# A paired feed-forward block: the chain behind a pair's products takes a step more, and SyncE's requests at the second group's start change places

## The chip, the cores and the metric

One NeuronCore of a Trainium2 chip runs the whole program in one launch. The metric is the device time of one execution in microseconds; for the kernel before, three runs gave a median of 971.46 us (970.23 to 972.13). Engines are named as in the profile: PE is TensorE (PEld its weight loads), DVE is VectorE, ACT is ScalarE, POOL is GpSimd, SP is SyncE, which here only issues DMAs.

## The reference

A macaron layer on 512 tokens of width 1024, in fp32: a feed-forward half step, a token mixer (differential and dilated attention), a second feed-forward half step, and a norm.

```
def swiglu(x, w_gate, w_up, w_down):
    return (jax.nn.silu(x @ w_gate) * (x @ w_up)) @ w_down
...
x = x + 0.5 * swiglu(rmsnorm(x, ffn1_norm[layer]), ffn1_w_gate[layer], ffn1_w_up[layer], ffn1_w_down[layer])
x = x + token_mixer(rmsnorm(x, mix_norm[layer]), ...)
x = x + 0.5 * swiglu(rmsnorm(x, ffn2_norm[layer]), ffn2_w_gate[layer], ffn2_w_up[layer], ffn2_w_down[layer])
return rmsnorm(x, final_norm)
```

The hidden width is 2816, that is 22 tiles of 128. The change lies in the two feed-forward stages alone; stage a is the first (its tiles end in a), stage b the second.

## The kernel before

**Numbers.** Every fp32 operand of a product is split into a high part, rounded to TensorE's fp32r format by a cast on ScalarE (`high`, L382), and a low part, the rest, made by a subtraction on VectorE (`low`, L386). A product of two operands is then three matmuls (`mm3`, L123 to L125): high by high, high by low, low by high.

**Tiles in pairs.** Of the 22 hidden tiles the first six (stage a) or four (stage b) are computed one at a time. From there two neighbours form a pair, and a pair's gate, its up product and later two tiles of the down product are each done with seven block products instead of eight, after Strassen and Winograd. One block product is twelve matmuls of 128x256. The seven of a unit and the PSUM bank that each writes (w, x, y or z) are the list `SEVEN`:

```
SEVEN = (("a11", "w", "b11"), ("s3", "z", "t3"), ("s2", "x", "t2"), ("a12", "w", "b21"),
         ("s1", "y", "t1"), ("a22", "x", "t4"), ("s4", "y", "b22"))
```

The weights' blocks a11, a12, a22 come from raw tiles (raw0, raw1). The sums s1 and s3 are formed by DMA: SyncE loads one block into a slot and GpSimd issues a second DMA that adds the other to it (`weight_sums`, L327). The sums s2 and s4 are VectorE's (`total`, L358). The blocks' own sums are carried through PSUM: after a11 ScalarE copies bank w into x, after s2 bank x into y (`product`, `put(starts[t + 1], A.copy, ...)`, in the profile at L411), and the later products add to them. So s1 can't start before the copy x to y is done. The block s4 writes y again, so it can't start before VectorE has read y for the second row (L414).

**Units.** `units` lists a stage's work in TensorE's order: the first gate pair, then gate and up of each further pair up to tile 12, five plain tiles of the down product ("p", over the unpaired tiles), the down product's first group of four units ("d"), then the pairs 14 to 20 (the second group), three plain tiles and the second group of d.

**The order of the other engines.** TensorE's order follows the list. VectorE's and ScalarE's (and SyncE's and GpSimd's in these stages) is written by a small event queue: every operation is put on a heap with a planned time and a rank, and the heap is emptied in order of time, then rank, then entry. A block product is planned at 1410 ns (`STEP`), a plain tile at 4080 ns. The planned times only make the order; on the chip each engine runs its list in order and waits on semaphores.

**Around a pair.** `pair_step` (L461) puts what follows each block. In a gate unit, ScalarE applies silu to bank w for g0's left half (after a12), VectorE adds to make both halves of g1 (after s1 and a22), ScalarE applies silu to g1 and to g0's right half. In the up unit VectorE multiplies g0 and g1 by the up product. g0 and g1 lie in a pool of two buffers (`ptb`), so the next pair's g0 takes the buffer of this one's and must wait for its last readers.

**The chain of T blocks.** `kept` (L499) turns a pair's g0 and g1 into what the down product reads. b11 and b2 are plain splits of g0's left half and of g1 (tiles h0, and h1 and h2). The T blocks need differences, made in place: two subtractions on g0 (`less`, L420), two on g1 (`stt`, L423), the second of each after the first. Then g0 is cast (tile h3, L550) and split (h4), and g1 is cast (h5, L558, called the second cast here) and split (h6). These run while TensorE is in the next pair's gate unit.

**Loads.** `pipeline` plans `weight_sums` of a unit 14 steps ahead of it and `load` (raw tiles, three buffers in rotation) seven steps ahead; where both fall on one time, the sums' rank is the lower and they come first. The sums lie in slots that the hidden tiles use too; those of gate 16 take slots that tile h2's rest and another of pair 8 held until the last unit of the first group d has read them.

Of the kernel before, what the change touches and what calls it, by code (L numbers as in the profile page):

```python
# [14 lines left out]
F32 = mybir.dt.float32  # L15
F32R = mybir.dt.float32r
I32 = mybir.dt.int32
AF = mybir.ActivationFunctionType
ALU = mybir.AluOpType
AX = mybir.AxisListType  # L20

P = 128
S = 512
# [20 lines left out]
PLAIN = 6  # L44
# [10 lines left out]
STEP, PLAIN_STEP = 1410, 4080  # L55
# [9 lines left out]
def tile_macaron(ctx: ExitStack, tc, xs, xT, wf, wgu1, wst1, wd1, wdg1, wqk, wv, wo, wgu2, wst2, wd2,  # L65
                 wdg2, lams, relb, onehot, addc, out):
    nc = tc.nc
    V, A, G, T = nc.vector, nc.scalar, nc.gpsimd, nc.tensor
# [4 lines left out]
    tp = ctx.enter_context(tc.tile_pool(name="tp", bufs=2))  # L73
# [124 lines left out]
    def ffn(wgu, wst, wd, wdg, n0, n1, norm, early, res, nm, hooks, ended, first=None,  # L198
# [90 lines left out]
        ups, up_w = {}, {}  # L289
        left, right = slice(0, HS), slice(HS, S)  # L290
# [11 lines left out]
        ops, begin, starts, now = [], {}, [], 0  # L302
# [25 lines left out]
        sums, raws, second, made, half, g, hs = {}, {}, {}, {}, [], {}, {}  # L328
# [72 lines left out]
        def at(time, rank, f, *a):  # L401
            count[0] += 1
            heapq.heappush(events, (time, rank, count[0], f, a))

        def put(time, f, *a):
            at(time, 0, f, *a)
# [6 lines left out]
        def add(o, a, b):  # L413
            V.tensor_tensor(o, a, b, op=ALU.add)  # L414

        def mul(o, a, b):
            V.tensor_tensor(o, a, b, op=ALU.mult)
# [46 lines left out]
        def pair_step(t, u, o, banks):  # L464
            j = u[1]
            pw, px, py, pz = (banks[b] for b in "wxyz")
            p7 = (sq if u[0] == "u" else res["bc"])[:, left]
            if o == "s3":
                put(t, A.copy, p7, pz)
            elif u[0] == "g":  # L470
                if o == "a12":
                    def first_block():
                        g[j] = [tp.tile([P, S], F32, tag="ptb", name=f"g{r}{nm}{j}")
                                for r in range(2)]
                        A.activation(g[j][0][:, left], pw, AF.Silu)

                    put(t, first_block)
                    if j == n1:
                        put(t + STEP, lambda: mul(g[j][0][:, left], ups[j][:, left],
                                                  g[j][0][:, left]))  # L480
                    return
                if o == "s2":
                    return
                g0, g1 = g[j]
                if o == "s1":
                    put(t, add, g1[:, right], py, p7)
                elif o == "a22":
                    put(t, add, g1[:, left], px, p7)
                    put(t + STEP * (j > n1),
                        lambda: A.activation(g1[:], g1[:], AF.Silu, scale=-1.0))  # L490
                elif o == "s4":
                    put(t, A.activation, g0[:, right], py, AF.Silu)
                    if j == n1:
                        put(t, mul, g1[:], ups[j + 1][:], g1[:])
                        put(t + STEP, mul, g0[:, right], ups[j][:, right], g0[:, right])
                        kept(j, t, t - 2 * STEP, t + STEP)
            else:
                g0, g1 = g[j]
                if o == "a12":  # L499
                    put(t, mul, g0[:, left], pw, g0[:, left])  # L500
                elif o == "s1":
                    put(t, add, sq[:, right], py, p7)
                elif o == "a22":
                    put(t, add, sq[:, left], px, p7)
                    put(t, stt, g1[:], sq[:], -1.0, g1[:], ALU.mult)
                elif o == "s4":
                    put(t, mul, g0[:, right], py, g0[:, right])
                    kept(j, t - STEP, t - 3 * STEP, t)

        def kept(j, t1, t0, t2):  # L510

            g0, g1 = g[j]

            def cast(o, a):
                A.copy(o, a)

            def rest(o, a, h):
                V.tensor_tensor(o, a, h.bitcast(F32), op=ALU.subtract)  # L520

            def parts(t, h, l, a):
                put(t, cast, h, a)
                put(t + STEP, rest, l, a, h)

            if j < PLAIN:
                for r, t in ((1, t1), (0, t2)):
                    h = ah[j + r] = slot(j + r, f"ah{nm}{j + r}", F32R)
                    l = al[j + r] = slot(JF + j + r, f"al{nm}{j + r}", F32R)
                    parts(t + STEP, h[:], l[:], g[j][r][:])  # L530
                return
            places = [lambda n=n, i=i: slot(i, f"h{n}{nm}{j}", F32R)
                      for n, i in enumerate(PAIR_SLOTS[(j - PLAIN) // 2 % 4])]
            t = {}

            def b11():
                t["b"] = places[0]()
                A.copy(t["b"][:, left], g0[:, left])

            def b2():  # L540
                t["h2"] = places[1]()
                A.copy(t["h2"][:], g1[:])

            def b2_rest():
                t["l2"] = places[2]()
                rest(t["l2"][:], g1[:], t["h2"][:])

            def t0_parts():
                t["h0"] = places[3]()
                A.copy(t["h0"][:], g0[:])  # L550

            def t0_rest():
                t["l0"] = places[4]()
                rest(t["l0"][:], g0[:], t["h0"][:])

            def t1_parts():
                t["h1"] = places[5]()
                A.copy(t["h1"][:], g1[:])  # L558

            def t1_rest():  # L560
                t["l1"] = places[6]()
                rest(t["l1"][:], g1[:], t["h1"][:])
                b = hs[j] = {"b11": (t["b"][:, left], t["b"][:, right])}
                for n, i, c in (("b21", 2, left), ("b22", 2, right), ("t1", 0, left),
                                ("t3", 0, right), ("t4", 1, left), ("t2", 1, right)):
                    b[n] = t[f"h{i}"][:, c], t[f"l{i}"][:, c]

            put(t0 + STEP, b11)
            put(t0 + 2 * STEP, lambda: rest(t["b"][:, right], g0[:, left], t["b"][:, left]))
            put(t1 + STEP, b2)  # L570
            n = max(t1, t2) + STEP
            put(n, b2_rest)
            put(n, less, g0[:, left], g0[:, left], g0[:, right])
            put(n, less, g0[:, right], g1[:, right], g0[:, right])
            put(n + STEP, t0_parts)
            put(n + STEP, stt, g1[:, right], g1[:, right], -1.0, g0[:, left], ALU.subtract)
            put(n + STEP, stt, g1[:, left], g1[:, right], -1.0, g1[:, left], ALU.subtract)
            put(n + STEP, t1_parts)
            put(n + 2 * STEP, t0_rest)
            put(n + 2 * STEP, t1_rest)  # L580

        def down_step(t, u, o, banks):
            _, group, m = u
# [20 lines left out]
        def pipeline():  # L604
            seen = {}
            for t, (u, o) in enumerate(ops):
                if o[0] == "p":
                    at(starts[t] - 2 * PLAIN_STEP, 1, load, u)
                    at(starts[t] - 2 * STEP, 3, high, t)
                    at(starts[t] - STEP, 2.5, low, t)  # L610
                else:
                    if t == begin[u]:
                        if u != units[0]:

                            time, s0 = starts[t] - 14 * STEP, sum_slots(u)
                            if s0 in seen:
                                time = max(time, starts[begin[seen[s0]] + 2])
                            seen[s0] = u
                            at(time, 1, weight_sums, u)
                        at(starts[t] - 7 * STEP, 1.5, load, u)  # L620
                    if o[0] in ("s2", "s4"):
                        at(starts[t] - 5 * STEP, 2, total, t)
                    at(starts[t] - 4 * STEP, 3, high, t)
                    at(starts[t] - 3 * STEP, 2.5, low, t)
                at(starts[t], 4, product, t)
            if bias is not None:
                at(starts[begin["p", 5]], 5, bias[0])
                at(starts[begin["d", 1, 0] + 2], 5, bias[1])
            up_weights(n1 + 1)
            for i in range(2):  # L630
                for k in up(n1 + i):
                    prepared(n1 + i, k)
                    run((8 * i + k - 15) * 680)
            run(1 << 40)
# [16 lines left out]
        for j in range(j0, n1):  # L651
# [9 lines left out]
            for hf in range(2):  # L661
                wh, wl = get_w(wgu[j, hf], f"gu{nm}{j}_{hf}")
                for kk in range(4):
                    k = hf * 4 + kk
                    for c, pt in ((0, pg), (1, pu)):
                        o = kk * 256 + c * P
# [34 lines left out]
    with tc.manual_schedule(engines={mybir.EngineType.DVE, mybir.EngineType.Activation}):  # L701
        for t in range(4):
            raw = wp.tile([P, 1024], F32, tag="raw", name=f"raw_f{t}")
            h, l = w_place()
            for kk in range(2):
# [18 lines left out]
                for j in range(2):  # L724
                    for c in range(2):
                        o = kk * 512 + (2 * j + c) * P
# [37 lines left out]
    n1 = {}  # L764
# [61 lines left out]
    at = {}  # L826
# [535 lines left out]
```

## Time and profile before

| | |
|---|---|
| median of three runs | 971.46 us (970.23 to 972.13) |
| the profiled execution, own time | 972.34 us |
| its span, first to last instruction | 970.6 us |
| granted TensorE clock, mean | 0.996 |
| DMA traffic | 136.71 MB, 141 GB/s mean |
| stage a, paired part | about 86 to 360 us |
| stage b, paired part | about 663 to 957 us |

The profile is of one execution. Its page has busy shares by engine; the view of waits has, for each engine, what it waited for, in total, how often, and the longest; the timeline has one row for each instruction: start, duration, engine, line, operation, out<-in, shape, and in brackets the engine's idle time ahead of it with what ended it. Instructions of one engine overlap at their ends, so the distance of two starts is shorter than a duration. A row whose engine is SPq is a DMA's issue, not its transfer.

### The profile page before, as it was taken

To read this page: it belongs to the slowest core of one execution; us is meant where nothing else is said; L and a number is where in the kernel's file an instruction comes from. 1 tells how busy PE (TensorE), PEld (TensorE's weight loads), DVE (VectorE), ACT (ScalarE), POOL (GpSimd) and SP (SyncE) were. 2 spreads that over 40 slices of the span, in tenths; PEclk is the share of its full clock that TensorE was granted. 3 is DMA by queue.
4 is the path that set the end of the run, shared out by engine and by line. 5 is a ranking of instruction groups with operands and counts; after the bars stand their busy time and mean duration, and the time that the engine had idled before them with its cause. 6 is when DMAs were issued, how large, how long until landed. Compare 5 with 4: busy or idle time off the path is not lost.

```text
span 970.6 us, 17197 instructions
## 1 busy us (share of the span) xinstructions
PE 938.2 (97%) x6452; PEld 867.4 (89%) x6452; DVE 725.6 (75%) x1490; ACT 535.5 (55%) x1102; POOL 98.2 (10%) x117
## 2 busy tenths in 40 slices
PE   9999999999999999999999999999999999999995
PEld 7789998999989998988989888889999899899895
DVE  6697887677887796668764546797787676887786
ACT  6455665355565575566756654455666344666462
POOL 0011100112102100000000003110210111210100
PEclk9999999999999999999999999999999999999998
DMA  7176645578746832444232214364772757874732
GB/s 258 46 198 150 153 120 157 140 185 230 164 122 172 219 104 87 130 118 122 88 109 89 67 38 133 111 172 112 185 169 84 186 153 193 211 172 110 179 110 87
DMA packets 60388, 136.71 MB, mean 141 GB/s; under 512 B 6848, under 2 KB 9152, under 8 KB 60304
## 3 DMA queue, kind: packets, MB, share of 16 engines
q1 hardware_dynamic: 46304, 110.14, 34.7%
q0 software_dynamic: 14000, 25.47, 16.7%
q8 instruction: 50, 0.82, 0.3%
q14 instruction: 34, 0.28, 0.1%
HBM read 130.30 MB, written 2.14 MB: 136 GB/s over the span
## 4 chain that ended last, share of the span: by engine, by line
PE 79%; DVE 13%; ACT 3%; issue 2%; DMA 2%; SPq 0%; DVEq 0%; ACTq 0%
DVE w L386 3%; PE po L1029 2%; PE pua L123 1%; PE pua L124 1%; PE pua L125 1%; PE pwo L123 1%; PE pwo L124 1%; PE pwo L125 1%; PE pv L889 1%; PE pv L887 1%; PE pv L888 1%; PE pt L1016 1%; PE pq L123 1%; PE pq L125 1%; PE pq L124 1%
## 5 line engine op out<-in xcount | busy, mean ns | idle before, releaser
L995 DVE CUSTOM_DVE_ANT_0 pr<-sc,strip 128x128 f32<-128x128 f32 (+3 forms) x64 | 30.8, 489 | 33.5 <-PE sc L993 32.6
L998 ACT ACTIVATE pr<-pr,mx 128x128 f32<-128x128 f32 (+3 forms) x64 | 36.0, 563 | 31.0 <-DVE mx L995 30.0
L382 ACT CAST w<-s2b 128x512 fp32r<-128x512 f32 x50 | 31.1, 622 | 17.6 <-DVE s2b L364 14.5
L386 DVE TENSOR_TENSOR w<-s2b,w 128x512 fp32r<-128x512 f32 x50 | 34.2, 685 | 8.0 <-ACT w L382 7.9
L382 ACT CAST w<-s2a 128x512 fp32r<-128x512 f32 x46 | 28.6, 622 | 18.6 <-DVE s2a L364 15.8
L1029 PEld LDWEIGHTS po<-v,ptb 128*128 128x128 f32 x240 | 32.7, 191 | 5.3 <-ACT ptb L1019 2.7
L150 POOL TENSOR_TENSOR sq<-sq,sqt 128x512 f32<-128x512 f32 x7 | 10.9, 1557 | 253.2 <-ACT sqt L149 253.2
L386 DVE TENSOR_TENSOR w<-s2a,w 128x512 fp32r<-128x512 f32 x46 | 31.5, 684 | 6.6 <-ACT w L382 6.6
L887 PE MATMUL pv<-w,xh 128*128 128x256 f32 x128 | 36.3, 283 | 0.0
L889 PE MATMUL pv<-w,xh 128*128 128x256 f32 x128 | 36.2, 283 | 0.0
L888 PE MATMUL pv<-w,xl 128*128 128x256 f32 x128 | 36.2, 283 | 0.0
L1029 PE MATMUL po<-v,ptb 128*128 128x64 f32 (+1 forms) x240 | 32.6, 269 | 1.8 <-ACT ptb L1019 1.7
L1019 ACT COPY ptb<-pt 128x128 f32<-128x128 f32 (+3 forms) x48 | 20.1, 424 | 20.2 <-PE pt L1016 19.9
L123 PE MATMUL pq<-xh,w 128*128 128x512 f32 x64 | 26.9, 421 | 0.0
L123 PE MATMUL pwo<-mh,w 128*128 128x512 f32 x64 | 25.6, 400 | 0.0
L124 PE MATMUL pq<-xl,w 128*128 128x512 f32 x64 | 25.1, 392 | 0.0
L123 PE MATMUL pk<-xh,w 128*128 128x512 f32 x64 | 25.1, 392 | 0.0
L125 PE MATMUL pq<-xh,w 128*128 128x512 f32 x64 | 25.1, 392 | 0.0
L125 PE MATMUL pk<-xh,w 128*128 128x512 f32 x64 | 25.0, 391 | 0.0
L124 PE MATMUL pwo<-ml,w 128*128 128x512 f32 x64 | 25.0, 391 | 0.0
L125 PE MATMUL pwo<-mh,w 128*128 128x512 f32 x64 | 25.0, 391 | 0.0
L124 PE MATMUL pk<-xl,w 128*128 128x512 f32 x64 | 25.0, 390 | 0.0
(661 smaller groups left out, 3993.1 us busy)
## 6 DMA issues: line engine op xcount, KB each, us to landing
raw_qk<-wqk_dram SPq DMA_DIRECT2D x16, 512.0 KB, 3.3
raw0bg<-wst_dram SPq DMA_DIRECT2D x9, 512.0 KB, 4.4
raw_gua<-wgu_dram SPq DMA_DIRECT2D x8, 512.0 KB, 3.4
raw0ag<-wst_dram SPq DMA_DIRECT2D x8, 512.0 KB, 4.5
raw0ad<-wdg_dram SPq DMA_DIRECT2D x8, 512.0 KB, 5.6
strip<-bias_rows SPq DMA_DIRECT2D x16, 256.0 KB, 3.6
raw_v<-wv_dram SPq DMA_DIRECT2D x8, 512.0 KB, 3.4
raw_wo<-wo_dram SPq DMA_DIRECT2D x8, 512.0 KB, 3.2
```

The source lines that it names most:

```text
L123: T.matmul(po, wh, mh, start=first, stop=False, skip_group_check=on)
L124: T.matmul(po, wh, ml, start=False, stop=False, skip_group_check=on)
L125: T.matmul(po, wl, mh, start=False, stop=last, skip_group_check=on)
L382: A.copy(made[t][0], source(t))
L386: V.tensor_tensor(l, source(t), h.bitcast(F32), op=ALU.subtract)
L887: T.matmul(po, xh[k][:, xs], wh[:, o:o + 256], start=k == 0, stop=False)
L888: T.matmul(po, xl[k][:, xs], wh[:, o:o + 256], start=False, stop=False)
L889: T.matmul(po, xh[k][:, xs], wl[:, o:o + 256], start=False, stop=k == KD - 1)
L995: V.tensor_tensor_reduce(out=pi, in0=ps[:, :w], in1=st["b"][m][:, w - 1::-1], op0=ALU.add, op1=ALU.min, scale=1.0, scalar=3.0e38, accum_ou ...
L998: A.activation(pi, pi, AF.Exp, scale=-1.0, bias=st["mx"][:, m, i:i + 1], accum_out=st["ls"][:, m, i:i + 1])
L1019: A.copy(ptb[:, :w], pt[:, :w])
L1029: T.matmul(st["po3"][:, i, d0:d0 + dn], st["ptb", m, i][:, k * P:(k + 1) * P], vt[u // 4, k][:, fo + d0:fo + d0 + dn], start=k == 0, stop= ...
```

## The change

Four things change in `ffn`, and no instruction is added or taken away.

1. The chain in `kept`: the first difference of g0 is planned one step earlier, the second cast (h5) a step later and at a rank behind the block product, that is behind the copies and casts planned for that time, and its rest (h6) a step later.
2. g0 and g1 of a pair are allocated at their first use instead of both with g0's first half, since the former pair's g1 is now read longer.
3. The casts and rests of the plain tiles are planned one step earlier.
4. The sums of gate 16 (`("g", PLAIN + 10)`) are planned a step later, so that the raw tiles of up 14 are requested ahead of them.

```
+            def tile(r):
+                if r not in g.setdefault(j, {}):
+                    g[j][r] = tp.tile([P, S], F32, tag="ptb", name=f"g{r}{nm}{j}")
+                return g[j][r]
...
-            n = max(t1, t2) + STEP
-            put(n, b2_rest)
+            n = max(t1, t2)
             put(n, less, g0[:, left], g0[:, left], g0[:, right])
-            put(n, less, g0[:, right], g1[:, right], g0[:, right])
-            put(n + STEP, t0_parts)
-            put(n + STEP, stt, g1[:, right], g1[:, right], -1.0, g0[:, left], ALU.subtract)
-            put(n + STEP, stt, g1[:, left], g1[:, right], -1.0, g1[:, left], ALU.subtract)
-            put(n + STEP, t1_parts)
-            put(n + 2 * STEP, t0_rest)
-            put(n + 2 * STEP, t1_rest)
+            put(n + STEP, b2_rest)
+            put(n + STEP, less, g0[:, right], g1[:, right], g0[:, right])
+            put(n + 2 * STEP, t0_parts)
+            put(n + 2 * STEP, stt, g1[:, right], g1[:, right], -1.0, g0[:, left], ALU.subtract)
+            put(n + 2 * STEP, stt, g1[:, left], g1[:, right], -1.0, g1[:, left], ALU.subtract)
+            put(n + 3 * STEP, t0_rest)
+            at(n + 3 * STEP, 5, t1_parts)
+            put(n + 4 * STEP, t1_rest)
...
                 if o[0] == "p":
                     at(starts[t] - 2 * PLAIN_STEP, 1, load, u)
-                    at(starts[t] - 2 * STEP, 3, high, t)
-                    at(starts[t] - STEP, 2.5, low, t)
+                    at(starts[t] - 3 * STEP, 3, high, t)
+                    at(starts[t] - 2 * STEP, 2.5, low, t)
...
+                            if u == ("g", PLAIN + 10):
+                                time += STEP
                             at(time, 1, weight_sums, u)
```

The rest of the diff writes the gate unit's steps with named helpers (`silu`, `second_row`, `times_up`) that issue the same instructions.

More of the change, by code (lines that the diff above doesn't have):

```diff
@@ L467, in pair_step, with silu, second_row, times_up @@
             p7 = (sq if u[0] == "u" else res["bc"])[:, left]
+            def tile(r):
+                if r not in g.setdefault(j, {}):
+                    g[j][r] = tp.tile([P, S], F32, tag="ptb", name=f"g{r}{nm}{j}")
+                return g[j][r]
+            def silu(r, c, p):
+                A.activation(tile(r)[:, c], p, AF.Silu)
+            def second_row(c, p):
+                add(tile(1)[:, c], p, p7)
+            def times_up(r, c):
+                mul(g[j][r][:, c], ups[j + r][:, c], g[j][r][:, c])
             if o == "s3":
@@ L471, in pair_step @@
                 if o == "a12":
[L472 to L477, printed above, removed]
-                    if j == n1:
[L479 to L486, printed above, removed]
+                    put(t, silu, 0, left, pw)
+                    if j == n1:
+                        put(t + STEP, times_up, 0, left)
+                elif o == "s1":
+                    put(t, second_row, right, py)
                 elif o == "a22":
-                    put(t, add, g1[:, left], px, p7)
-                    put(t + STEP * (j > n1),
-                        lambda: A.activation(g1[:], g1[:], AF.Silu, scale=-1.0))
+                    put(t, second_row, left, px)
+                    put(t + STEP * (j > n1), lambda: A.activation(
+                        g[j][1][:], g[j][1][:], AF.Silu, scale=-1.0))
                 elif o == "s4":
-                    put(t, A.activation, g0[:, right], py, AF.Silu)
+                    put(t, silu, 0, right, py)
                     if j == n1:
-                        put(t, mul, g1[:], ups[j + 1][:], g1[:])
-                        put(t + STEP, mul, g0[:, right], ups[j][:, right], g0[:, right])
+                        put(t, times_up, 1, slice(0, S))
+                        put(t + STEP, times_up, 0, right)
                         kept(j, t, t - 2 * STEP, t + STEP)
             else:
-                g0, g1 = g[j]
+                g0, g1 = g[j][0], g[j][1]
                 if o == "a12":
@@ L510, in kept @@
         def kept(j, t1, t0, t2):
-            g0, g1 = g[j]
+            g0, g1 = g[j][0], g[j][1]
             def cast(o, a):
```

## The prediction

> **What bounds the kernel now.** First the page's totals: TensorE is busy 97% of the span. Busy is a duration and matmuls overlap, so this is no proof that nothing is left; what counts is where TensorE's starts fall apart. So next the view of waits, TensorE's alone, whose columns are total us, times, longest.
>
> ```profile
> PE 938.2 (97%) x6452; PEld 867.4 (89%) x6452; DVE 725.6 (75%) x1490; ACT 535.5 (55%) x1102; POOL 98.2 (10%) x117
> ```
> ```profile
> PE pyga L123 <- ACT pyga L411: 6.8, 6, 1.2
> PE pygb L123 <- ACT pygb L411: 6.8, 6, 1.1
> ...
> PE pygb L123 <- DVE g1b L414: 0.9, 1, 0.9
> ...
> PE pda L125 <- DVE w L386: 0.4, 2, 0.2
> PE pdb L125 <- DVE w L386: 0.4, 2, 0.2
> PE pyga L123 <- DVE g1a L414: 0.4, 1, 0.4
> ```
>
> All three kinds lie in the two feed-forward stages, the only code that the change moves. Twelve times, once in each gate unit that follows another pair, TensorE waits about 1.1 us for ScalarE's copy of bank x into bank y; twice for VectorE to have read bank y; four times for the low half of a plain tile's weights. What one wait costs is read from the starts, here TensorE's in the second pair of stage a (columns: start, duration, then what it is).
>
> ```profile
> 116.36 0.28 PE L123 MATMUL pyua<-xh,w 128*128 128x256 f32 x1
> ```
> ```profile
> 123.34 0.28 PE L125 MATMUL pwga<-xh,w 128*128 128x256 f32 x1
> 124.74 0.38 PE L123 MATMUL pyga<-txa,w 128*128 128x256 f32 x1 [1.12 <-ACT pyga L411]
> 124.97 0.28 PE L124 MATMUL pyga<-tta,w 128*128 128x256 f32 x1
> ...
> 127.69 0.28 PE L123 MATMUL pyga<-xh,w 128*128 128x256 f32 x1
> ```
>
> From 116.36 (s4 of the pair's up unit) to the last start of a12 at 123.34 are 59 steps, so one matmul starts every 0.1183 us and a block of twelve takes 1.42. The start after the wait comes 1.40 later and the one behind it 0.23 later: 1.28 + 0.11 = 1.39 us lost, the shown gap plus 0.27. By the same rule the two waits on g1 cost 0.4 + 0.27 and 0.9 + 0.27, 1.8 together, and each of the four plain ones 0.2 + 0.27 = 0.47.
>
> Why the copy is late is seen on ScalarE, then VectorE, in the same pair.
>
> ```profile
> 121.01 0.62 ACT L550 CAST h3a<-g0a 128x512 fp32r<-128x512 f32 x1 [0.71 <-DVE g0a L420]
> 123.01 0.62 ACT L558 CAST h5a<-g1a 128x512 fp32r<-128x512 f32 x1 [1.38 <-DVE g1a L423]
> 123.53 0.36 ACT L411 COPY rbc_n<-pzga 128x256 f32<-128x256 f32 x1
> 123.80 0.62 ACT L382 CAST w<-s2a 128x512 fp32r<-128x512 f32 x1
> 124.31 0.38 ACT L411 COPY pyga<-pxga 128x256 f32<-128x256 f32 x1
> 124.62 0.61 ACT L382 CAST w<-raw0au 128x512 fp32r<-128x512 f32 x1
> ```
> ```profile
> 116.56 0.42 DVE L414 TENSOR_TENSOR sq<-pxua,sq 128x256 f32<-128x256 f32 x1 [0.28 <-PE pxua L125]
> ...
> 120.10 0.42 DVE L420 TENSOR_TENSOR g0a<-g0a 128x256 f32<-128x256 f32 x1
> 120.55 0.42 DVE L420 TENSOR_TENSOR g0a<-g1a,g0a 128x256 f32<-128x256 f32 x1
> 120.89 0.68 DVE L366 TENSOR_TENSOR s2a<-raw0ag,s2a 128x512 f32<-128x512 f32 x1
> ...
> 122.55 0.42 DVE L423 SCALAR_TENSOR_TENSOR g1a<-g1a 128x256 f32<-128x256 f32 x1
> ...
> 123.49 0.68 DVE L520 TENSOR_TENSOR h4a<-g0a,h3a 128x512 fp32r<-128x512 f32 x1
> 124.10 0.68 DVE L520 TENSOR_TENSOR h6a<-g1a,h5a 128x512 fp32r<-128x512 f32 x1
> ...
> 126.51 0.41 DVE L414 TENSOR_TENSOR g1a<-pyga,rbc_n 128x256 f32<-128x256 f32 x1
> ```
>
> ScalarE stands idle 1.38 us in front of the second cast (h5), which needs both rows of g1 from VectorE, done at 122.97. Three short instructions queue behind it, the copy into y last.
>
> **The change part by part.** The order of both programs, engine by engine, gives: TensorE and GpSimd unchanged; on ScalarE the cast h5 goes behind the y copy and the cast of the up unit's raw0; on VectorE the first difference goes two or three places forward, h6 one back, and around the plain tiles the weights' low halves go forward; on SyncE the requests of the up unit of pair 14 (raw0, raw1) go ahead of the sums of gate 16, in both stages. No instruction is added or taken away.
>
> *The y copy, eleven pairs.* New walk of ScalarE with the row's own pitches: h3 at 121.01 (its input is g0's second difference; the first one's earlier place does not make that earlier, since the same instructions stand ahead of it), rbc_n 121.53, the cast of s2 121.80 (its sum is done at 121.57), the y copy 0.51 later at 122.32 and done at 122.70. Unstalled, block a12 ends its starts at 123.34 and s1 begins at 123.45. So the copy is 0.75 early and 1.39 us goes.
>
> What is late next: s4 writes bank y again and must wait until VectorE has read it (the kind of wait that the profile already has on g1). s4 would start seven blocks after 116.36: 126.30. VectorE reads y from 126.51 to 126.92 now. Can that come earlier? The stretch from 116.56, where VectorE last waits for TensorE, to that end is one solid queue:
>
> ```profile
> 116.56:126.93 10.37, 9.25 (x78) 9.04 (x77) 10.27 (x21) 6.58 (x14) 0.86 (x1) 1.00 0.55 152
> ```
>
> (the fourth number is VectorE: 10.27 busy of 10.37.) The change keeps the same instructions ahead of the read. Their order adds one back-to-back dependence (the first difference behind g0's product) and removes one (the second behind the first: pitch 0.45 against 0.34), so the sum stays. h6 needs h5: h5 now runs from 123.10 (behind raw0's cast, with g1 done) to 123.72, and h6 moves to 124.70, so nothing waits there. The silu into g0's other buffer must wait for h4's end at 124.17; behind it stands the cast of s3, to 125.1, read at 126.84. Hence y is free at 126.92, TensorE starts 0.05 later, as it does behind the y copy (124.69 to 124.74); that is 0.67 after 126.30, and with the 0.11 of the slow first matmul 0.78 is lost in the new place. **Gain 1.39 - 0.78 = 0.61 a pair, 6.7 us for eleven.** In the up unit VectorE has idle time (0.28 at 116.56), so it starts each pair level again. Bounds: the exchanged dependence may cost or give 0.11 a pair (1.2 us in all); from below a gain of 1.39 a pair, if the read of y were no limit.
>
> The Trainium skill (Perfetto Trace Analysis, "Tensor Engine Instruction") says that ScalarE and VectorE take their instructions strictly in order. That speaks against this change: the read of y cannot pass h6. By it 0.61 stands; without it 1.39.
>
> *The first pair of stage a.* There the order is another: h5 stands behind the silu and the cast of s3 as well, and h6 behind the up unit's sum and raw0.
>
> ```profile
> 103.01 0.68 DVE L520 TENSOR_TENSOR h4a<-g0a,h3a 128x512 fp32r<-128x512 f32 x1
> ...
> 105.42 0.42 DVE L414 TENSOR_TENSOR g1a<-pyga,rbc_n 128x256 f32<-128x256 f32 x1
> ```
>
> The silu waits for h4 (103.69), the cast of s3 follows at 104.0, h5 runs 104.5 to 105.15, h6 from 105.2 and the read of y from 105.8 to 106.2, 0.4 later than now. Unstalled s4 would be due at 104.93, so the loss is about as large as the present one. **I credit 0**; bounds 0 to 0.4.
>
> *Plain tiles.* VectorE makes the first plain tile's low half last, behind the pair's products:
>
> ```profile
> 157.68 0.42 DVE L414 TENSOR_TENSOR sq<-pyua,sq 128x256 f32<-128x256 f32 x1 [0.99 <-PE pyua L125]
> 159.10 0.42 DVE L414 TENSOR_TENSOR sq<-pxua,sq 128x256 f32<-128x256 f32 x1 [1.00 <-PE pxua L125]
> 159.56 0.69 DVE L423 SCALAR_TENSOR_TENSOR g1a<-sq,g1a 128x512 f32<-128x512 f32 x1
> 160.17 0.95 DVE L386 TENSOR_TENSOR w<-raw0ap,w 128x768 fp32r<-128x768 f32 x1
> ```
>
> Now it stands between the two sq rows, from 158.0 to 158.97, inside the 1.00 us in which VectorE waits for TensorE anyway: 159.10 is not moved. TensorE needs it only from 160.3. **Gain 4 x 0.47 = 1.9 us.** The later plain tiles' casts come a step earlier on engines that have room. The pair's own T blocks end a step later, but three or five plain tiles (4.08 us each in the planner's count) stand ahead of the down units that read them: nothing.
>
> *Raw tiles of the second group.* SyncE's queue in stage a and what it does to VectorE:
>
> ```profile
> 214.00 0.38 SPq L337 DMA_DIRECT2D s3au<-wst_dram  x1
> 220.43 0.33 SPq L337 DMA_DIRECT2D s1ag<-wst_dram  x1
> ...
> 221.53 0.70 SPq L346 DMA_DIRECT2D raw0au<-wst_dram  x1
> 222.96 0.33 SPq L346 DMA_DIRECT2D raw1au<-wst_dram  x1
> ```
> ```profile
> 225.03 0.69 DVE L386 TENSOR_TENSOR w<-s2a,w 128x512 fp32r<-128x512 f32 x1 [0.72 <-ACT w L382]
> 228.39 0.69 DVE L364 TENSOR_TENSOR s2a<-s1au,raw0au 128x512 f32<-128x512 f32 x1 [2.67 <-DMA raw0au<-wst_dram]
> ```
>
> SyncE holds s1ag until its slot is free at 220.4, and raw0au stands behind it, so VectorE waits 2.67 us for it and reads y late. In front of the sums raw0au goes out at 214.4, when s3au is off; even with the 6.8 us that it takes here (221.53 to about 228.3) it lands at 221.2, four us before 225.6, where VectorE wants it. **Gain 1.8 us.** In return the sums of gate 16 leave after raw1au, from about 223.3, three us later. Each is a load and an accumulating copy, one after the other; at 5 to 6.4 us apiece (an estimate, just under raw0au's 6.8) the one that is cast first lands at 233.8 to 236.6. It is wanted 0.6 before its present time:
>
> ```profile
> 236.88 0.62 ACT L382 CAST w<-s3ag 128x512 fp32r<-128x512 f32 x1
> ```
>
> That is close: bounds 0 to 2 us lost over both stages. The Trainium skill (DMA: Bandwidth & Descriptors, "Issuing engines are not separate DMA queues") says that requests of all engines share the same DMA engines; by it raw0au's earlier bytes delay the up unit's own sums, which no row here prices.
>
> **Sum:** 6.7 + 0 + 1.9 + 1.8 = 10.4 us. The profiled execution took 972.34 us (span 970.6), 0.88 above the median 971.46 of the runs shown; it would take 961.9, and I forecast **961.1** for the median.
>
> **Rivals.** *Full gain*: the read of y does not hold s4, because VectorE gets through earlier. For it: VectorE is idle a quarter of the span. Against: 10.27 of 10.37. It adds 11 x 0.78 = 8.6: 952.5. Chance 0.06. *The pairs give nothing*: in all pairs h5, and with it h6 and the read of y, slides by 0.6, as in the first pair. Against: the walk leaves h5 done 0.98 before h6. 971.46 - 3.7 = 967.8, chance 0.07. *The raw tiles' gain is given back*: sums of gate 16 late by up to 2 us: 963, chance 0.09. *Slower*: one mechanism, h6 in VectorE's queue. h5 now stands behind the cast of raw0, which waits for a DMA; h6 waits for h5, the read of y for h6, s4 for the read, eleven times. It starts when h5 ends after 124.70 (walk: 123.72) and takes 11 us for each us; from 10.4/11 = 0.95 later, 125.65, the kernel is slower, at 1 us more 982. Against: raw0 shows no DMA wait in the ordinary pairs. Chance 0.07. *The change does not do what it says* is excluded for the order, which both programs show.
>
> **How the numbers follow.** Forecast 0.71, the others as given. The range takes the forecast, its bounds (1.2 on the pairs either way, 2 on the sums, the runs' own 1 us) and the late sums: 957.5 to 965.0; left out are the two far gains or none and the loss, 0.20. A measurement of this kernel can tell about 0.2%, 2 us. Faster by more: 0.71 + 0.09 + 0.06 and most of the 0.07 at 967.8, 0.91; within: 0.02; slower: 0.07.
>
> **What would show it.** Right: the rows of TensorE waiting for ScalarE's y copy are gone but for the first pair's place, and a row of eleven or twelve waits for VectorE's g1 stands in their place, 0.5 us each; the plain tiles' rows and the wait for raw0 are gone; a pair takes 20.7 us instead of 14 x 1.42 + 1.39 = 21.3. Wrong: no waits on g1 (full gain), waits of over 1 us on g1 with VectorE idle before h6 (the queue), or waits of ScalarE on a DMA before the cast of s3 in gate 16.

## The result and the profile after

The changed kernel takes 960.6 us (median of 4, 959.39 to 961.46) against 970.85 us before in the same comparison: a ratio of 0.9893, 95% interval 0.9874 to 0.9912, some 10.3 us less. The forecast was 961.1.

The page's line of busy times, and the view of TensorE's waits:

```profile
PE 937.5 (98%) x6452; PEld 867.9 (90%) x6452; DVE 725.1 (76%) x1490; ACT 535.6 (56%) x1102; POOL 98.4 (10%) x117
```
```profile
PE pyga L123 <- DVE g1a L414: 3.9, 6, 1.3
PE pygb L123 <- DVE g1b L414: 3.1, 6, 0.5
```

Busy times are those of before to within 0.7 us; what differs is TensorE's gaps. The rows for the y copy (L411) and for the plain tiles' low halves (L386) are gone. In their place stand twelve waits for VectorE's read of y: eleven of 0.5 us and one of 1.3. Lines behind the diff have moved by 6 to 11 (the second cast is now L564).

The pair that the prediction walked through, first TensorE, then ScalarE, then VectorE:

```profile
121.59 0.28 PE L125 MATMUL pwga<-xh,w 128*128 128x256 f32 x1
121.71 0.28 PE L123 MATMUL pyga<-txa,w 128*128 128x256 f32 x1
...
124.43 0.28 PE L125 MATMUL pxga<-tta,w 128*128 128x256 f32 x1
125.23 0.39 PE L123 MATMUL pyga<-xh,w 128*128 128x256 f32 x1 [0.52 <-DVE g1a L414]
125.45 0.28 PE L124 MATMUL pyga<-xl,w 128*128 128x256 f32 x1
```
```profile
120.57 0.38 ACT L411 COPY pyga<-pxga 128x256 f32<-128x256 f32 x1
120.87 0.62 ACT L382 CAST w<-raw0au 128x512 fp32r<-128x512 f32 x1
121.39 0.62 ACT L564 CAST h5a<-g1a 128x512 fp32r<-128x512 f32 x1
122.52 0.39 ACT L476 ACTIVATE g0a<-pwga 128x256 f32<-128x256 f32 x1 [0.51 <-DVE h4a L526]
```
```profile
114.81 0.42 DVE L414 TENSOR_TENSOR sq<-pxua,sq 128x256 f32<-128x256 f32 x1 [0.28 <-PE pxua L125]
...
122.95 0.68 DVE L526 TENSOR_TENSOR h6a<-g1a,h5a 128x512 fp32r<-128x512 f32 x1
...
124.76 0.41 DVE L414 TENSOR_TENSOR g1a<-pyga,rbc_n 128x256 f32<-128x256 f32 x1
```

Block s1 (121.71) now follows a12 (121.59) without a gap, the y copy being done at 120.95. Block s4 starts 0.80 after a22's last start instead of 0.118: 0.68 lost there, and 0.10 at the slow first matmul (0.22 to the next start), 0.78 together. VectorE's read begins 9.95 us after its last wait for TensorE (114.81 to 124.76), as it did before (116.56 to 126.51).

Where the time went shows between the first start of a stage's first gate and the last start of its last down block, here the four ends of before and then of after (stage a, stage b):

```profile
86.48 0.28 PE L123 MATMUL pwga<-xh,w 128*128 128x256 f32 x1
...
359.50 0.28 PE L125 MATMUL pyda<-h1a,w 128*128 128x256 f32 x1
...
663.51 0.28 PE L123 MATMUL pwgb<-xh,w 128*128 128x256 f32 x1
...
956.67 0.28 PE L125 MATMUL pydb<-h1b,w 128*128 128x256 f32 x1
```
```profile
84.53 0.28 PE L123 MATMUL pwga<-xh,w 128*128 128x256 f32 x1
...
353.04 0.28 PE L125 MATMUL pyda<-h1a,w 128*128 128x256 f32 x1
...
658.63 0.28 PE L123 MATMUL pwgb<-xh,w 128*128 128x256 f32 x1
...
945.97 0.28 PE L125 MATMUL pydb<-h1b,w 128*128 128x256 f32 x1
```

Stage a went from 273.02 to 268.51 us, stage b from 293.16 to 287.34: 4.5 and 5.8, 10.3 together. What lies outside the stages (86.48 to 84.53 ahead, 304.0 to 305.6 between) was not touched; it differs from execution to execution. So the experiments are judged by stage length beside their times. A stage length is read from one profiled execution. The times come from three comparisons, each with runs of the kernel before: it took 970.85 us beside the changed kernel, 970.78 beside the chain alone, both kernels with the cast moved and the sum alone behind the read, and 969.98 beside the other four. A time is best compared with the kernel before of its own comparison.

| kernel | time, us | stage a | stage b |
|---|---|---|---|
| before | 970.85 | 273.02 | 293.16 |
| changed | 960.6 | 268.51 | 287.34 |
| chain alone | 964.5 | 270.30 | 289.28 |
| plain tiles alone | 969.28 | 272.31 | 291.23 |
| requests alone | 969.75 | 272.38 | 291.99 |
| cast back in front | 966.14 | 271.35 | 291.00 |
| cast later | 965.9 | 271.02 | 290.39 |
| sum behind the read | 954.15 | 265.49 | 283.74 |
| sum and low half behind | 953.21 | 264.63 | 282.65 |
| the same, first pair's cast too | 950.83 | 263.05 | 282.65 |

### The profile page after: what moved, and what is told of

Its sections match the earlier page's. It is cut to its first block, busy times and chain, and to the rows that moved or that the text cites. A ratio compares the mean times of both kernels' runs of the same rounds, so it can differ in the third digit from the quotient of the medians.

```text
span 959.6 us, 17173 instructions
## 1 busy us (share of the span) xinstructions
PE 937.5 (98%) x6452; PEld 867.9 (90%) x6452; DVE 725.1 (76%) x1490; ACT 535.6 (56%) x1102; POOL 98.4 (10%) x117
## 4 chain that ended last, share of the span: by engine, by line
PE 80%; DVE 15%; issue 2%; ACT 1%; DVEq 0%; POOL 0%; POOLq 0%
DVE w L386 5%; PE po L1040 2%; PE pua L123 1%; PE pua L124 1%; PE pua L125 1%; PE pwo L123 1%; PE pwo L124 1%; PE pwo L125 1%; PE pv L900 1%; PE pv L898 1%; PE pv L899 1%; PE pt L1027 1%; PE pq L123 1%; PE pq L125 1%; PE pq L124 1%
## 5 line engine op out<-in xcount | busy, mean ns | idle before, releaser
L386 DVE TENSOR_TENSOR w<-s2b,w 128x512 fp32r<-128x512 f32 x50 | 34.2, 685 | 7.9 <-ACT w L382 7.9
L386 DVE TENSOR_TENSOR w<-s2a,w 128x512 fp32r<-128x512 f32 x46 | 31.4, 683 | 6.5 <-ACT w L382 6.5
```

The source lines that it names most:

```text
L386: V.tensor_tensor(l, source(t), h.bitcast(F32), op=ALU.subtract)
```

## The experiments

**The chain alone.** The changed kernel with the plain tiles and the requests as before.

```
-                    at(starts[t] - 3 * STEP, 3, high, t)
-                    at(starts[t] - 2 * STEP, 2.5, low, t)
+                    at(starts[t] - 2 * STEP, 3, high, t)
+                    at(starts[t] - STEP, 2.5, low, t)
...
-                                time += STEP
+                                time += 0
```

> The chain's part alone (plain tiles and SyncE's order as before). Theory (the second cast held up the y copy; VectorE's read of y is the next limit): eleven waits of 1.39 us become eleven of 0.78, the first pair of stage a gives nothing, the plain tiles' four waits and the two waits for raw0 stay: 6.6 us less than before, about 964.5. Rival (most of the gain came from the plain tiles and the requests, or the parts only work together): 3 us or less.

Measured: 964.5 us, ratio to before 0.9935 (0.9917 to 0.9954); the stages are 2.7 and 3.9 shorter, 6.6 together. TensorE's waits (fourteen for g1: eleven of the pairs, the first pair's, and the two behind raw0):

```profile
PE pyga L123 <- DVE g1a L414: 4.4, 7, 1.3
PE pygb L123 <- DVE g1b L414: 3.8, 7, 0.7
...
PE pdb L125 <- DVE w L386: 0.4, 2, 0.2
PE pda L125 <- DVE w L386: 0.4, 2, 0.2
```

The chain carries two thirds of the gain, and by itself.

**The cast back in front of the copy**, everything else as changed.

```
-            at(n + 3 * STEP, 5, t1_parts)
+            put(n + 2 * STEP, t1_parts)
```

> The changed kernel with the second cast put back ahead of the y copy on ScalarE; the first difference stays early, VectorE's order stays as changed. Theory: the cast's place is the whole pair gain, so the twelve waits for the y copy of 1.39 us are back and those for VectorE go: 6.5 us more than the changed kernel, about 967. Rival (the earlier first difference carries the gain): about 961.

Measured: 966.14 us, 0.9957 (0.9943 to 0.9972) of before; the stages are 2.8 and 3.7 longer than the changed kernel's, 6.5 together.

```profile
PE pyga L123 <- ACT pyga L411: 6.9, 6, 1.2
PE pygb L123 <- ACT pygb L411: 6.8, 6, 1.1
```

These are before's rows again, though the first difference is still early: that part of the chain's edit did nothing, and the place of one cast on ScalarE is the pairs' gain.

**The cast one place later**, behind the silu, in all pairs but stage a's first.

```
-            at(n + 3 * STEP, 5, t1_parts)
-            put(n + 4 * STEP, t1_rest)
+            if j == n1:
+                at(n + 3 * STEP, 5, t1_parts)
+                put(n + 4 * STEP, t1_rest)
+            else:
+                at(n + 4 * STEP, 0.5, t1_parts)
+                at(n + 4 * STEP, 0.7, t1_rest)
```

> The changed kernel with the second cast one instruction later on ScalarE, behind g0's silu, in all pairs but the first of stage a. Theory (strict order on VectorE: the cast's rest waits for the cast, the read of y for the rest): the cast ends 0.5 us after the place of its rest, so each of eleven pairs loses 0.5 more: 5.7 us more, about 966. Rival (there is room between the rest and the read, or the read may go ahead): no change, 960.6.

Measured: 965.9 us, 5.3 more than the changed kernel; stages 2.5 and 3.1 longer. VectorE, then TensorE's waits:

```profile
123.77 0.69 DVE L526 TENSOR_TENSOR h6a<-g1a,h5a 128x512 fp32r<-128x512 f32 x1 [0.41 <-ACT h5a L564]
124.38 0.68 DVE L364 TENSOR_TENSOR s2a<-s1au,raw0au 128x512 f32<-128x512 f32 x1
...
125.59 0.41 DVE L414 TENSOR_TENSOR g1a<-pyga,rbc_n 128x256 f32<-128x256 f32 x1
```
```profile
PE pyga L123 <- DVE g1a L414: 6.5, 6, 1.3
PE pygb L123 <- DVE g1b L414: 6.2, 6, 1.0
```

VectorE stands idle at h6 for the cast, and 0.5 us arrives at TensorE in each of eleven pairs. This is the mechanism of the prediction's slower rival, with its price of 11 us for each us; one instruction more in front of the cast costs more than half of what the change brought.

**A sum behind the read of y.** On VectorE the up unit's s2 goes behind the read.

```
-                        at(starts[t] - 5 * STEP, 2, total, t)
+                        at(starts[t] - (4 if o[0] == "s2" and u[0] == "u" else 5) * STEP, 2, total, t)
```

> The changed kernel with VectorE's sum s2 of the up unit (0.60 us in its queue) behind the read of y instead of ahead of it. Theory (what stands ahead of the read in VectorE's order sets the new wait): y is free 0.60 earlier, the loss of a pair falls from 0.78 to about 0.18, eleven times: 6.6 us less, about 954; the first pair, whose read waits for the second cast, gains nothing. Rival (the wait is set by something that comes later, not by the queue): no change, 960.6.

Measured: 954.15 us, 0.9829 (0.9814 to 0.9845) of before, 6.4 less than the changed kernel's time; the stages are 3.0 and 3.6 shorter, 6.6 together. One row of waits on g1 is left, the first pair's:

```profile
PE pyga L123 <- DVE g1a L414: 1.3, 1, 1.3
```

The other eleven blocks s4 still lose 0.18 us each by TensorE's starts, as forecast; the view does not list gaps so short. So the length of VectorE's queue ahead of the read set the new wait: 0.60 us out of the queue took 0.60 off the loss.

**Two instructions behind the read**, the same and the low half of the up unit's raw0.

```
-                    at(starts[t] - 3 * STEP, 2.5, low, t)
+                    at(starts[t] - (2 if o[0] == "a11" and u[0] == "u" else 3) * STEP, 2.5, low, t)
```

> The changed kernel with two of VectorE's instructions, the up unit's sum s2 and its low half of raw0 (0.60 us each), behind the read of y. Theory: y is free 1.2 us earlier, 0.53 ahead of need, so eleven waits go wholly: 11 x 0.78 = 8.6 us less than the changed kernel, about 952, some 2 us below the kernel with the sum alone behind. Rival (the low half comes too late for block a11 of the up unit, or TensorE is held elsewhere): no better than 954.

Measured: 953.21 us, 0.9825 (0.981 to 0.984) of before; stages 3.9 and 4.7 shorter than the changed kernel's, 8.6 together, which is the eleven waits whole. Against the kernel before it in the table the stages are 1.9 shorter, which is the 0.18 of eleven pairs. VectorE's read of y now stands right behind h6, and is done at 123.92, 0.39 us before s4 starts (VectorE, then TensorE):

```profile
122.71 0.68 DVE L526 TENSOR_TENSOR h6a<-g1a,h5a 128x512 fp32r<-128x512 f32 x1
123.50 0.42 DVE L414 TENSOR_TENSOR g1a<-pyga,rbc_n 128x256 f32<-128x256 f32 x1
123.84 0.68 DVE L364 TENSOR_TENSOR s2a<-s1au,raw0au 128x512 f32<-128x512 f32 x1
```

```profile
124.31 0.28 PE L123 MATMUL pyga<-xh,w 128*128 128x256 f32 x1
```

From h6's start to the read's are 0.79 us, where VectorE's instructions of this size otherwise follow after 0.60, so y is free 0.2 later than the forecast's 1.2 us promised. This is no wait for TensorE: the same 0.79 stands between h6 and the read in the changed kernel's first pair (shown below), where the last matmul of s1 had started 2.5 us before the read. The read writes g1, and in the pool of two buffers that is the buffer which h6 reads; that this makes the step longer is likely, but no run tried it.

**And the first pair's cast.**

```
-            at(n + 3 * STEP, 5, t1_parts)
+            at(n + (2 if j == n1 else 3) * STEP, 5, t1_parts)
```

> As the kernel with two instructions behind the read of y, and in the first pair of stage a the second cast ahead of g0's silu, as in the other pairs. Theory: the first pair's loss, 1.60 us in the changed kernel, goes too: 10.2 us less than the changed kernel, about 950.4. Rival (the first pair is held by VectorE's queue and not by the cast): as the kernel without the second edit, about 952.

Measured: 950.83 us, 0.9802 (0.9786 to 0.9818) of before. Against the kernel without the second edit stage a is 1.58 shorter and stage b the same, as the first pair's 1.60 says; the view lists no wait of TensorE on bank y any more. This version beats both kernels: it takes 19.2 us less than before in the same comparison, and its stages are 10.2 us shorter than the changed kernel's (5.5 and 4.7).

**The plain tiles alone**, on the kernel before.

```
-                    at(starts[t] - 2 * STEP, 3, high, t)
-                    at(starts[t] - STEP, 2.5, low, t)
+                    at(starts[t] - 3 * STEP, 3, high, t)
+                    at(starts[t] - 2 * STEP, 2.5, low, t)
```

> The kernel before with the plain tiles' casts and rests one step earlier, nothing else. Theory: the four waits of TensorE for a plain tile's low half go, 1.9 us, about 969.0 beside 970.9, which is at the edge of what times can tell; the profile tells it: no row of TensorE waiting for L386. Rival (the low half in front of the pair's sums delays these and the blocks behind them): the rows go, and new waits of the same size come.

(This kernel and the next also allocate g0 and g1 at first use, as the changed one does, part 2 of the change; the rows for the y copy stay those of before, 6.9 and 6.8 us, so that part gains nothing alone.)

Measured: 969.28 us, 0.9985 (0.9975 to 0.9995) of before, so 0.5 to 2.4 us less. No row of TensorE waiting for L386 is left. The stages are 0.7 and 1.9 shorter, and not 0.95 each, because one thing besides differed in this execution: the waits behind raw0, which the edit doesn't touch. Before they were 0.4 us in stage a and 0.9 in stage b. Here the one in stage a is longer, and the view lists none for stage b:

```profile
PE pyga L123 <- DVE g1a L414: 0.6, 1, 0.6
```

**The requests alone**, on the kernel before.

```
+                            if u == ("g", PLAIN + 10):
+                                time += STEP
                             at(time, 1, weight_sums, u)
```

> The kernel before with the raw tiles of up 14 requested ahead of the sums of gate 16, nothing else. Theory: the two waits for VectorE's g1 at pair 14 go, 1.8 us, about 969.0; raw0's landing is no longer waited for by VectorE. Rival (gate 16's sums, three us later, come late): a new wait in pair 16, on a DMA or on VectorE or ScalarE behind one, of 0 to 2 us, so no change of time.

Measured: 969.75 us, 0.9992 (0.9983 to 1.0): 0 to 1.6 us less, which does not settle it by the times. The trace has no wait on g1 any more, and the stages are 0.6 and 1.2 shorter, 1.8 together. The rival's mechanism is there too, without its price:

```profile
234.60 0.62 ACT L382 CAST w<-s3ag 128x512 fp32r<-128x512 f32 x1 [0.41 <-DMA s3ag<-wst_dram]
235.85 0.62 ACT L382 CAST w<-s2a 128x512 fp32r<-128x512 f32 x1 [0.63 <-DVE s2a L364]
```

The sum of gate 16 is 0.41 us late for ScalarE, which then waits 0.63 for VectorE's s2, where the kernel before waits 1.14: the lateness is taken out of idle time. Since the waits behind raw0 vary from execution to execution (0.4 and 0.9 before, 0.6 and none listed with the plain tiles alone), one profile does not price them; what their removal is worth in the median stays open, and by the times it is 0 to 1.6 us.

## Why the prediction was right, point by point

*The y copy, eleven pairs: 6.7 us.* Measured 6.6 with the chain alone (of which the first pair takes back 0.1); by TensorE's starts each of the eleven lost 1.39 and now loses 0.78. Walk and trace agree to a few hundredths: copy 0.75 early (0.76 in the trace), h6 unmoved, y read at the same place in VectorE's queue, 0.78 lost at s4 (0.78). The walk was right because it asked what was late next.

*Strict order on VectorE.* The rule of the Trainium skill (Perfetto Trace Analysis, "Tensor Engine Instruction"), by which a ready instruction does not pass one that waits, agrees with the kernel with the cast one place later: while VectorE stood idle 0.41 us for h6, the sum s2, which reads nothing that h6 or the cast makes, stayed behind it and started only 0.61 after it. The read of y is no clean test of the rule, since it writes the buffer that h6 reads and must follow h6 in any order.

*The first pair: 0.* The path was right, h5 behind the silu and the cast of s3, then h6, then the read; one step was too short. The pair lost 1.60 us instead of 1.48, and was credited 0. VectorE, then ScalarE:

```profile
102.27 0.69 DVE L386 TENSOR_TENSOR w<-raw0au,w 128x512 fp32r<-128x512 f32 x1
103.29 0.69 DVE L526 TENSOR_TENSOR h6a<-g1a,h5a 128x512 fp32r<-128x512 f32 x1 [0.33 <-ACT h5a L564]
104.08 0.42 DVE L414 TENSOR_TENSOR g1a<-pyga,rbc_n 128x256 f32<-128x256 f32 x1
```
```profile
102.64 0.62 ACT L564 CAST h5a<-g1a 128x512 fp32r<-128x512 f32 x1
```

h6 waits 0.33 for the cast, as the walk has it, but the read follows h6 after 0.79 where the walk took 0.6. The stated bounds, 0 to 0.4, do not say whether they mean a gain or a loss; the loss was 0.1.

*Plain tiles: 1.9 us.* The low half is where it was put, in front of the second sq row, in time that was idle:

```profile
154.72 0.42 DVE L414 TENSOR_TENSOR sq<-pyua,sq 128x256 f32<-128x256 f32 x1 [0.99 <-PE pyua L125]
155.06 0.95 DVE L386 TENSOR_TENSOR w<-raw0ap,w 128x768 fp32r<-128x768 f32 x1
156.15 0.42 DVE L414 TENSOR_TENSOR sq<-pxua,sq 128x256 f32<-128x256 f32 x1
```

*Raw tiles: 1.8 us.* SyncE's order and what VectorE does with it, in the changed kernel:

```profile
210.47 0.41 SPq L337 DMA_DIRECT2D s3au<-wst_dram  x1
210.98 0.38 SPq L346 DMA_DIRECT2D raw0au<-wst_dram  x1
219.42 0.33 SPq L346 DMA_DIRECT2D raw1au<-wst_dram  x1
219.84 0.44 SPq L337 DMA_DIRECT2D s1ag<-wst_dram  x1
```
```profile
222.11 0.69 DVE L364 TENSOR_TENSOR s2a<-s1au,raw0au 128x512 f32<-128x512 f32 x1
...
224.84 0.42 DVE L414 TENSOR_TENSOR g1a<-pyga,rbc_n 128x256 f32<-128x256 f32 x1 [1.22 <-PE pyga L125]
```

raw0au goes out right behind s3au; VectorE's sum no longer waits and its read of y waits for TensorE. As a difference of two traces the term came out (the requests alone: 1.8); as a difference of medians it is smaller. The prediction took one execution's 0.4 and 0.9 for all of them. The delay that shared DMA engines might have caused the up unit's own sums did not show at VectorE.

*The signs.* The expected rows came: eleven waits of 0.5 us on g1 (the first pair's row for the y copy, which was to stay, is gone too), none on raw0, none for the plain tiles' low halves, a pair in 20.66 us (from one s4, at 125.23, to the next, at 145.89). Two of the signs named as wrong showed too, and neither cost what it stood for. The wait of over 1 us with VectorE idle ahead of h6 is the first pair's alone. And in stage b ScalarE waits for a DMA ahead of the cast of s3 in gate 16:

```profile
826.74 0.63 ACT L382 CAST w<-s3bg 128x512 fp32r<-128x512 f32 x1 [0.80 <-DMA s3bg<-wst_dram]
```

The sums are late there, as the rival on the raw tiles had it, but TensorE has no wait behind them. The walk had called this close, and it was.

*The sum.* 10.4 was forecast, the stages give 10.3, the medians 10.25. Of the rivals, the slower one and the full gain are now both measured as edits: half a microsecond later at h6 costs 5.6 in the stages, and a queue shorter by two instructions with the first pair's cast brings 10.2 in the stages. That the medians differ by the forecast gain to within 0.2 us is in part luck: they are of four runs each, and the single runs spread over 2 us.

## What to carry to other kernels

When a wait of the bound engine goes, walk on to the next thing that it needs from the same bank, and measure how full the other engine's queue is between its last wait and that point: if it is busy throughout, the queue's length sets the new wait. Then look in that queue for instructions whose results are wanted later, and put them behind; here two of 0.6 us each took 8.6 us more out of the stages, beside the 10.3 of the whole change. A wait that depends on a DMA's landing needs more than one execution before it is priced.

## What the runs showed of the hardware

The part between the stages, the same in all kernels, took 304.0 us in some profiles and 305.6 in others. The difference goes with the granted clock behind one wait in the mixer, 1.7 us long (here the changed kernel, TensorE's timeline and two stretches; the number behind POOL's is the clock):

```profile
547.91 1.10 PE L1040 MATMUL po<-v,ptb 128*128 128x64 f32 x8 [1.70 <-ACT ptb L1030]
```
```profile
546.00:549.40 3.40, 1.70 (x12) 1.41 (x12) 1.93 (x4) 2.94 (x6) 0.00 (x0) 1.00 0.00 0
549.50:552.90 3.40, 3.40 (x12) 2.81 (x11) 1.58 (x7) 0.92 (x4) 0.00 (x0) 0.50 0.39 136
```

After it the clock was 0.50 for one stretch of 3.4 us in six of the ten profiles, at a cost of 1.6 us, and 1.00 throughout in the other four, before among them; the wait is there in all ten. The Trainium skill (TensorE: Matmul & The Clock Gate, "Part 1: The HAM clock gate") gives about 3.4 us of idle time for the fall; here it fell with no longer gap than 1.7 us ahead of it in TensorE's rows. What decides whether it falls stays open. The two profiles that the result rests on differ in this, so the change's effect in them is 10.3 in its own stages, whatever the spans say.
